# Other prices in a list scheduler, and a lock for VectorE and GpSimd: a two-layer decoder trunk on one core

## The chip, the core and the metric

The kernel runs on one NeuronCore of a Trainium2 chip. Five engines work side by side, each with its own queue, in order: TensorE (PE; its weight loads are listed as PEld), VectorE (DVE), ScalarE (ACT), GpSimd (POOL) and SyncE (SP), which issues most of the DMAs. The metric is the time of one execution on the device, in microseconds, lower is better. TensorE's clock has two levels, 2.4 and 1.2 GHz; the profile shows the granted share of the first (1.00 or 0.50, or a mean of them).

## What is computed

A batch of one sequence of 512 tokens, with 16 meta tokens ahead of it, goes through two layers, in float32, width 1024. A layer is a feed-forward network (half weight), a mixer, and a second feed-forward network, each followed by a layer norm on the residual:

```python
h = _layer_norm(ALPHA * h + 0.5 * _swiglu(h, wg0, wu0, wd0), g0, b0)      # 1024 -> 2816 -> 1024
lru_u, lru_y, ssd_z, ssd_xbc, ssd_dt, dn_qkv, ... = split(h @ w_in)       # 1024 -> 2832
mix = concat([rg_lru(...), mamba2_ssd(...), gated_deltanet(...)]) @ w_out
h = _layer_norm(ALPHA * h + mix, g1, b1)
h = _layer_norm(ALPHA * h + 0.5 * _swiglu(h, wg1, wu1, wd1), g2, b2)
```

The three parts of the mixer are recurrences over the tokens: the gated delta rule and the SSD in chunks of 64, with a state that is handed from chunk to chunk, the RG-LRU as a scan. The meta tokens are dropped from the output.

## The kernel before, in words

The tokens are worked in two halves: half 0 has 272 (16 meta, 256 others), half 1 has 256. Activations lie with the features on the partitions. A float32 product is made of three matmuls in a faster format, with weights and activations split into a high and a low part (`gemm`): high by high, low by high, high by low. These are the "g" matmuls, 128 x 128 weights by 256 or 272 columns, 24 for each product of 1024 inputs; in the trace `g<-hh,wt`, `g<-hl,wt` and `g<-hid,wt`. A weight slab of 512 KB is loaded to `wr` by SP, its high part cast by ACT, and the low part subtracted by POOL (in four pieces of 128 x 256) or by DVE (one of 128 x 1024), all into a tile `wt`.

The mixer's other matmuls are small and in plain float32; they write tiles "c". Per half they come as follows. `times` makes the step sizes (`dt_g`, `st_adt`) from a projection and its transposes (`sm`, `smd`, `mt`). `dn_pre`, `dn_solve`, `dn_post` and `dn_scan` do the delta rule: per-block matrices (`db`, `d_blk`), a triangular solve on DVE, its extension by blocks (`d_c`, `db`), and a scan with the state `d_s` (`d_r`, `d_wv`). `ssd_block` does the SSD: transposes of `acc`, decay matrices from `st_adt` and `tri`, masks on DVE, ACT and POOL (tiles `s`), and sums into `acc` and the state `s_st`. `lru` holds two gate matmuls (`wgate`, `l_h`) and the scan. `dn_finish` and `ssd_finish` normalise (`d_sq`, `s_sv`, `lq`). `layer_norm` sums the columns with a matmul of ones by `ls`, centres and squares on DVE, ACT and POOL (`ls2`, `lq`), sums the squares, takes a reciprocal square root in a chain of small DVE operations on `lv`, spreads the result with matmuls `ident,lv`, and writes `hh` and `hl`.

To keep PE at work, `Trunk.program` runs half 0's mixer beside half 1's feed-forward network, and the other way round, in an order given by a table (`KNOTS`, in `weave`). That order is only the recording: the calls go to a `Recorder`, whose queues hold operations with the tiles that they read and write. `levels` gives each operation the length of the longest priced path behind it. `schedule` then plays the five engines by the prices: it picks the engine that can start first, and on it the operation that is ready in the plan with the lowest class and the longest path; a "c" operation on PE and the operations around the PSUM tiles stand in the class ahead of the g matmuls. A result counts as usable on another engine after a lag from a table (`LAG`, plus `MARGIN`). PE's price doubles in the plan where its own count of columns says that the clock is low, and in long pauses it plans filler matmuls of ones. The order that comes out is issued to the engines as it is (`manual_schedule`), so each engine works it off in that order on the chip, and waits where the plan was wrong.

The prices are in `price`, per engine and kind of operation. In the profile of this kernel all operations have the line L390, in which the recorder issues them, and the fillers L388.

## Time and profile before

| | us |
|---|---|
| median of 3 runs (lowest to highest) | 2460.74 (2446.69 to 2464.13) |
| the profiled execution | 2460.38 |
| its span, first to last instruction | 2458.7 |
| PE busy in the span | 2312.6 (94%) |
| DVE / ACT / POOL busy | 1504.2 / 865.9 / 883.0 |
| mean granted clock of TensorE | 0.948 |

The feed-forward stretches lie from 0 to about 370, from 890 to 1560 and from 2090 us on; the first layer's mixer lies from about 370 to 890 us and the second's from 1560 to 2090. A busy PE is not a PE at its peak, since matmuls are pipelined and their ends are modelled. A wait is put down to the operation that came last.

### The profile page before, as it was taken

To read this page: it belongs to the slowest core of one execution; us is meant where nothing else is said; L and a number is where in the kernel's file an instruction comes from. 1 tells how busy PE (TensorE), PEld (TensorE's weight loads), DVE (VectorE), ACT (ScalarE), POOL (GpSimd) and SP (SyncE) were. 2 spreads that over 40 slices of the span, in tenths; PEclk is the share of its full clock that TensorE was granted. 3 is DMA by queue.
4 is the path that set the end of the run, shared out by engine and by line. 5 is a ranking of instruction groups with operands and counts; after the bars stand their busy time and mean duration, and the time that the engine had idled before them with its cause. 6 is when DMAs were issued, how large, how long until landed. Compare 5 with 4: busy or idle time off the path is not lost.

```text
span 2458.7 us, 46832 instructions
## 1 busy us (share of the span) xinstructions
PE 2312.6 (94%) x18712; PEld 2199.1 (89%) x18712; DVE 1504.2 (61%) x3529; ACT 865.9 (35%) x1546; POOL 883.0 (36%) x1214
## 2 busy tenths in 40 slices
PE   8999998988899999999999999998989989999997
PEld 8999998876887999999999999988768878999996
DVE  6444467757867664444574444678577686654445
ACT  3222344442333454222242223443433444432222
POOL 5000566634545576000010005666445556640000
PEclk9999999987886999999999999999888989999999
DMA  6232454531341456233232334545314525552320
GB/s 169 78 103 87 131 145 144 146 97 35 110 108 54 139 157 186 86 104 95 68 95 80 91 91 138 156 139 141 97 35 118 142 61 155 172 168 90 91 90 35
DMA packets 426332, 271.99 MB, mean 111 GB/s; under 512 B 33421, under 2 KB 407921, under 8 KB 425857
## 3 DMA queue, kind: packets, MB, share of 16 engines
q1 hardware_dynamic: 425536, 268.83, 37.7%
q8 instruction: 147, 2.41, 0.4%
q0 software_dynamic: 576, 0.16, 0.1%
q14 instruction: 73, 0.59, 0.1%
HBM read 260.76 MB, written 8.19 MB: 109 GB/s over the span
## 4 chain that ended last, share of the span: by engine, by line
PE 70%; DVE 16%; DMA 4%; issue 3%; POOL 3%; ACT 3%; SPq 0%; POOLq 0%; DVEq 0%; ACTq 0%
PE g L390 61%; PE c L390 9%; POOL wt L390 2%; DVE wt L390 2%; DVE acc L390 2%; DVE fs L390 1%; DVE lru L390 1%; ACT wt L390 1%; DMA wr<-in_ffn_w_gate_dram 1%; DVE d_sq L390 1%; DVE s L390 1%; DMA wr<-in_ffn_w_up_dram 1%; DMA d_tx<-d_xd 1%; DVE sp L390 1%; DVE l_h L390 1%
## 5 line engine op out<-in xcount | busy, mean ns | idle before, releaser
L390 PE MATMUL g<-hh,wt 128*128 128x256 f32 (+1 forms) x7616 | 1063.7, 290 | 22.5 <-DVE fs L390 8.8
L390 PEld LDWEIGHTS g<-hh,wt 128*128 128x128 f32 x7616 | 985.4, 192 | 37.5 <-DVE fs L390 9.0
L390 POOL TENSOR_TENSOR wt<-wr,wt 128x256 fp32r<-128x256 f32 x884 | 681.8, 803 | 783.7 <-ACT wt L390 726.4
L390 ACT CAST wt<-wr 128x1024 fp32r<-128x1024 f32 x484 | 498.0, 1040 | 619.0 <-PE g L390 482.0
L390 PE MATMUL g<-hl,wt 128*128 128x256 f32 (+1 forms) x3808 | 562.7, 288 | 1.8 <-DVE hl L390 1.2
L390 PE MATMUL g<-hid,wt 128*128 128x256 f32 (+1 forms) x4224 | 543.7, 286 | 18.6 <-DVE hid L390 10.2
L390 PEld LDWEIGHTS g<-hid,wt 128*128 128x128 f32 x4224 | 524.4, 189 | 27.2 <-DVE hid L390 13.0
L390 PEld LDWEIGHTS g<-hl,wt 128*128 128x128 f32 x3808 | 505.3, 192 | 6.3 <-DVE hl L390 2.5
L390 DVE SCALAR_TENSOR_TENSOR acc<-g,acc 128x256 f32<-128x256 f32 (+1 forms) x608 | 256.7, 427 | 226.1 <-PE g L390 222.0
L390 DVE TENSOR_TENSOR wt<-wr,wt 128x1024 fp32r<-128x1024 f32 x263 | 335.0, 1285 | 88.1 <-ACT wt L390 86.8
L390 DVE SCALAR_TENSOR_TENSOR fs<-ft,g 128x272 f32<-128x272 f32 (+1 forms) x200 | 84.6, 423 | 188.8 <-ACT ft L390 188.0
L390 DVE TENSOR_TENSOR g<-fs,g 128x256 f32<-128x256 f32 (+1 forms) x176 | 76.4, 434 | 173.9 <-PE g L390 173.5
L390 ACT ACTIVATE ft<-g 128x272 f32<-128x272 f32 (+1 forms) x208 | 80.6, 388 | 281.6 <-PE g L390 249.2
L390 ACT CAST hid<-g 128x256 fp32r<-128x256 f32 (+1 forms) x176 | 65.8, 374 | 223.5 <-DVE g L390 223.2
L390 POOL TENSOR_TENSOR ls<-ls,lq 128x256 f32<-128x256 f32 (+1 forms) x30 | 27.6, 920 | 264.2 <-ACT lq L390 261.3
L390 DVE TENSOR_TENSOR hid<-g,hid 128x256 fp32r<-128x256 f32 (+1 forms) x176 | 74.9, 425 | 42.4 <-ACT hid L390 42.1
L390 POOL TENSOR_TENSOR wr<-wr,db 128x512 f32<-128x512 f32 x4 | 5.0, 1274 | 262.0 <-ACT wr L390 262.0
L390 DVE SCALAR_TENSOR_TENSOR fs<-g,par,fs 128x271 f32<-128x271 f32 (+1 forms) x144 | 69.1, 482 | 21.9 <-ACT halo L390 17.0
L390 ACT ACTIVATE fs<-g,par 128x272 f32<-128x272 f32 (+1 forms) x48 | 25.2, 524 | 67.4 <-PE g L390 57.9
L390 DVE SCALAR_TENSOR_TENSOR acc<-acc,par,c 128x256 f32<-128x256 f32 (+1 forms) x104 | 43.6, 480 | 8.6 <-PE c L390 8.5
L390 ACT ACTIVATE ft<-fs 128x272 f32<-128x272 f32 (+1 forms) x56 | 23.7, 423 | 58.6 <-DVE fs L390 58.6
L390 POOL TENSOR_TENSOR s<-s,s_sm 128x512 f32<-128x512 f32 (+1 forms) x20 | 22.0, 1105 | 61.6 <-ACT s L390 45.1
(305 smaller groups left out, 1742.4 us busy)
## 6 DMA issues: line engine op xcount, KB each, us to landing
wr<-in_ffn_w_gate_dram SPq DMA_DIRECT2D x120, 512.0 KB
wr<-in_ffn_w_up_dram SPq DMA_DIRECT2D x120, 512.0 KB
wr<-in_ffn_w_down_dram SPq DMA_DIRECT2D x120, 512.0 KB
wr<-in_w_in_dram SPq DMA_DIRECT2D x88, 512.0 KB
wr<-in_w_out_dram SPq DMA_DIRECT2D x32, 512.0 KB
res<-acc SPq DMA_DIRECT2D x2, 1088.0 KB
acc<-res SPq DMA_DIRECT2D x8, 272.0 KB
acc<-in_x_dram SPq DMA_DIRECT2D x4, 512.0 KB
```

The costliest lines, as they stand in the source:

```text
L390: op.fn(*[on(x) for x in op.args], **{k: on(x) for k, x in op.kw.items()})
```

## The change

The prices of the plan change, and the plan gets one more rule. A matmul costs 12.5 ns beside its columns instead of 2.5 (`GAP`); in the half-clock case the columns alone double. A DMA is planned at 300 bytes per ns instead of 360. The lag from PE to ACT is 225 ns instead of 197. New is a lock: `shares` says which operations use the way into SBUF that DVE and POOL share: all of POOL's but memsets and DMAs, and on DVE those with more than one input tensor in SBUF (scalars not counted) and the copies, memsets and operations with a scalar that have all operands in SBUF. When such an operation is placed, the other engine's may start, in the plan, no sooner than its end less 90 ns (POOL behind DVE) or 160 ns (DVE behind POOL); until then it goes back and another ready operation is taken. Nothing else changes; no instruction of the program is added or removed, except that 57 fillers are planned and not 59.

```diff
--- before.py
+++ after.py
@@ -56,7 +56,7 @@
 class Op:
 
 
-    __slots__ = ("eng", "fn", "args", "kw", "cost", "load", "done", "cls", "prev", "preds", "succs", "level", "left", "ready", "seq", "tiles", "cols", "start", "after")
+    __slots__ = ("eng", "fn", "args", "kw", "cost", "load", "done", "cls", "prev", "preds", "succs", "level", "left", "ready", "seq", "tiles", "cols", "start", "after", "port")
 
 
 class Slots:
@@ -84,9 +84,9 @@
 
 
     PE, DVE, ACT, POOL, SP = range(5)
-    TICK, FULL, PAIR = 10240 / 3, 0.3735, 40
+    TICK, FULL, PAIR, GAP = 10240 / 3, 0.3735, 40, 12.5
     LAG = (
-        (0, 196, 197, 196, 189),
+        (0, 196, 225, 196, 189),
         (60, 127, 128, 155, 120),
         (210, 142, 142, 165, 135),
         (110, 76, 75, 104, 87),
@@ -125,14 +125,14 @@
         n = self.size(a[0])
         if name == "dma_start":
             b = n * a[0].ap[0][1] * 4
-            return (1040 if eng == self.POOL else 475), b / 360.0
+            return (1040 if eng == self.POOL else 475), b / 300.0
         if eng == self.PE:
             w, x = (a[1], a[2])
             fast = w.dtype == F32R
             c = (1 if fast else 2 if name == "transpose" else 4) / 2.4
             if self.region(a[0])[0] and self.size(w) <= 64:
                 return self.PAIR, 55
-            return self.size(x) * c + 2.5, self.size(w) * c
+            return self.size(x) * c + self.GAP, self.size(w) * c
         wide = max(self.size(x) for x in a)
         psum = any(x.space == bass.MemoryType.PSUM for x in a)
         if eng == self.DVE:
@@ -149,6 +149,15 @@
             return 36 + 0.85 * n * (2 if name == "affine_select" else 1), 0
         return (120 + 3.33 * n if name == "tensor_copy" else 148 + 2.1 * n), 0
 
+    def shares(self, eng, name, args):
+
+        sb = [x.space != bass.MemoryType.PSUM for x in args if hasattr(x, "ap") and self.size(x) > 1]
+        if eng == self.POOL:
+            return name not in ("memset", "dma_start")
+        if eng != self.DVE:
+            return False
+        return sum(sb[1:]) > 1 or name in ("tensor_scalar", "tensor_copy", "memset") and all(sb)
+
     def add(self, eng, name, fn, args, kw):
 
         t = args[0].tensor.name
@@ -168,7 +177,8 @@
         op = Op()
         op.eng, op.fn, op.args, op.kw, op.cls, op.seq = eng, fn, args, kw, self.cls, len(self.ops)
         op.cost, op.load = self.price(eng, name, args, kw)
-        op.cols = (op.cost - 2.5) * args[1].ap[0][1] / P if eng == self.PE and op.cost != self.PAIR else 0
+        op.cols = (op.cost - self.GAP) * args[1].ap[0][1] / P if eng == self.PE and op.cost != self.PAIR else 0
+        op.port = self.shares(eng, name, args)
         op.preds, op.tiles = set(), set()
         outs = [args[0]] + ([kw["accum_out"]] if kw.get("accum_out") is not None else [])
         ins = [x for x in list(args[1:]) + list(kw.values()) if hasattr(x, "ap")]
@@ -274,6 +284,7 @@
         lags = [[g + m for g, m in zip(r, MARGIN)] for r in self.LAG]
         free, now = [0.0] * 5, [0.0] * 5
         last_load = dma = 0.0
+        port = [0.0] * 5
         busy = [self.TICK] + [0.0] * 2000
         pending = [[] for _ in range(5)]
         ready = [[] for _ in range(5)]
@@ -302,6 +313,9 @@
                 op = self.ops[heapq.heappop(pending[e])[1]]
                 heapq.heappush(ready[e], (key(op), op.seq))
             op = self.ops[heapq.heappop(ready[e])[1]]
+            if op.port and port[e] > s:
+                heapq.heappush(pending[e], (port[e], op.seq))
+                continue
             new = [t for t in op.tiles if t not in owned]
             if new:
                 assert len(new) == 1
@@ -332,13 +346,16 @@
                         t += w
                 c, w = op.cost, op.load
                 if busy[int((s + w) // self.TICK)] < self.FULL * self.TICK:
-                    c, w = 2 * c, 2 * w
+                    c, w = 2 * (c - (self.GAP if op.cost != self.PAIR else 0)), 2 * w
                 op.start = s = max(s, last_load + w, op.ready + w)
                 last_load = s
                 busy[int(s // self.TICK) + 1] += op.cols
                 s += c - op.cost
             end = s + op.cost
             free[e] = end
+            if op.port:
+                q, early = (self.POOL, 90) if e == self.DVE else (self.DVE, 160)
+                port[q] = end - early
             if op.fn.__name__ == "dma_start":
                 dma = max(dma, end + 650) + op.load
                 end = dma
```

The operations come out in another order on all engines. On PE, in the first layer's mixer, half 0, from the fillers (`ones`) ahead of the end of the layer norm of half 1 (`lv`) into the SSD blocks (`acc`, `st_adt`). The numbers behind c_ and g_ are buffers. Before:

```order
L388 MATMUL c_123<-ones_104 128x128 x2
L390 MATMUL c_123<-ident_96,lv_876 128x128 x2
L390 MATMUL c_121<-ident_96,acc_24_119 16x128 x4
L390 MATMUL c_122<-ident_96,acc_24_119 16x128
L390 MATMUL c_122<-acc_24_119 16x16
L390 MATMUL c_123<-acc_24_119 16x16
L390 MATMUL c_121<-tri_105,st_adt_635 128x16 x2
L390 MATMUL c_122<-tri_105,st_adt_635 128x16
```

With the change, from the end of the same layer norm (the line number of the issue is L407):

```order
L407 MATMUL c_122<-ident_96,lv_876 128x128 x2
L407 MATMUL c_121<-ident_96,acc_24_119 16x128 x4
L407 MATMUL c_123<-ident_96,acc_24_119 16x128
L407 MATMUL c_123<-acc_24_119 16x16
L407 MATMUL g_145<-hl_4_99,wt_142 128x272 x5
L407 MATMUL g_136<-hh_2_97,wt_156 128x272 x16
L407 MATMUL g_136<-hl_4_99,wt_156 128x272 x8
L407 MATMUL c_122<-acc_24_119 16x16
L407 MATMUL g_139<-hh_2_97,wt_135 128x272 x15
L407 MATMUL c_121<-tri_105,st_adt_635 128x16 x2
L407 MATMUL c_123<-tri_105,st_adt_635 128x16
```

Before, the next g matmul comes behind all of the SSD blocks' 89 matmuls; with the change 125 g matmuls stand among them. Between the layer norm's first matmul (`c<-ls,ones`) and `lv` stand 116 g matmuls before, 27 with the change.

On PE, in the second layer's mixer, half 1, where the delta rule's scan (`d_wv`) ends and the SSD blocks begin. Before:

```order
L390 MATMUL g_139<-hh_3_98,wt_135 128x256 x6
L390 MATMUL c_123<-tri_105,st_adt_998 128x128 x4
L390 MATMUL g_139<-hh_3_98,wt_135 128x256 x4
L390 MATMUL g_139<-hl_5_100,wt_135 128x256 x5
L390 MATMUL c_125<-ls_565,ones_104 128x256
L390 MATMUL g_139<-hl_5_100,wt_135 128x256 x3
L390 MATMUL g_136<-hh_3_98,wt_156 128x256
L390 MATMUL c_124<-s_814_909,s_st_907 64x128
L390 MATMUL c_124<-s_808_903,s_799_894 64x128
```

With the change:

```order
L407 MATMUL c_125<-ident_96,acc_32_127 128x128
L407 MATMUL c_125<-acc_32_127 128x128
L407 MATMUL c_124<-acc_32_127 128x128
L407 MATMUL c_121<-tri_105,st_adt_998 128x128 x4
L407 MATMUL c_123<-d_wv_760,db_652 64x64 x2
L407 MATMUL g_136<-hh_3_98,wt_156 128x256 x2
L407 MATMUL g_136<-hl_5_100,wt_156 128x256 x3
L407 MATMUL c_125<-ls_565,ones_104 128x256
L407 MATMUL c_124<-s_814_909,s_st_907 64x128
L407 MATMUL c_124<-s_808_903,s_799_894 64x128
```

Here g matmuls went out from between the small ones: from the first `d_c` matmul of this half to its layer norm's end (`lv`) 131 stand before, 62 with the change, and 40 more of them stand ahead, between `dt_g` and `d_c`. Three more counts of the same kind, on PE: between the first mixer's transposes of step sizes (`sm`) and `dt_g`, 82 g matmuls before and 171 with the change; among the SSD blocks of the second mixer's half 0, 12 and 73; over the layer norm ahead of these, 130 and 82.

## Rows read from the trace of the kernel before

**Rows 1.** The page: its first line, the span and the instructions in it.

```profile
span 2458.7 us, 46832 instructions
```

**Rows 2.** The stretches of 100 us (busy time and count of each engine; granted clock; DMA).

```profile
500.00:600.00 100.00, 88.53 (x662) 68.87 (x662) 64.83 (x166) 36.10 (x81) 35.23 (x48) 0.81 0.20 54
1100.00:1200.00 100.00, 100.00 (x821) 100.00 (x820) 45.39 (x81) 23.09 (x38) 0.00 (x0) 1.00 0.30 90
1900.00:2000.00 100.00, 92.28 (x840) 78.99 (x838) 69.36 (x196) 39.73 (x78) 53.98 (x71) 0.91 0.39 104
```

**Rows 3.** The page, section 4: the chain that ended last, by engine.

```profile
PE 70%; DVE 16%; DMA 4%; issue 3%; POOL 3%; ACT 3%; SPq 0%; POOLq 0%; DVEq 0%; ACTq 0%
```

**Rows 4.** Stretches of the first mixer, 517 to 590 us, and their sum.

```profile
530.00:545.00 15.00, 8.89 (x64) 8.19 (x65) 12.09 (x30) 8.19 (x19) 6.64 (x10) 0.80 0.52 141
545.00:560.00 15.00, 13.14 (x55) 9.14 (x55) 8.52 (x31) 5.03 (x12) 3.50 (x5) 0.50 0.20 70
560.00:575.00 15.00, 15.00 (x51) 8.10 (x51) 6.25 (x13) 1.41 (x4) 1.47 (x3) 0.50 0.00 1
575.00:590.00 15.00, 12.09 (x78) 8.81 (x78) 12.50 (x30) 3.55 (x7) 5.72 (x6) 0.95 0.00 1
sum 73.00, PE 62.11 PEld 46.71 DVE 46.14 ACT 25.66 POOL 24.93; mean PE 12.42 PEld 9.34 DVE 9.23 ACT 5.13 POOL 4.99
```

**Rows 5.** Timeline of PE (start, length, operation, count), the layer norm's first matmul.

```profile
517.22 0.70 PE L390 MATMUL c<-ls,ones 128*128 128x256 f32 x2
```

**Rows 6.** Timeline of PE, the same layer norm's last matmuls.

```profile
537.17 0.71 PE L390 MATMUL c<-ident,lv 128*128 128x128 f32 x4 [2.25 <-DVE lv L390]
```

**Rows 7.** Timeline of PE, another layer norm, its first and last matmuls.

```profile
1245.65 0.63 PE L390 MATMUL c<-ls,ones 128*128 128x256 f32 x2
1258.76 0.71 PE L390 MATMUL c<-ident,lv 128*128 128x128 f32 x4 [0.60 <-DVE lv L390]
```

**Rows 8.** Timeline of DVE, the operations on lv (3 elements a partition).

```profile
532.73 1.15 DVE L390 TENSOR_SCALAR lv<-lv 128x3 int32<-128x3 int32 x2
533.91 0.65 DVE L390 TENSOR_TENSOR lv<-lv 128x3 f32<-128x3 f32 x1
534.60 1.33 DVE L390 SCALAR_TENSOR_TENSOR lv<-lv 128x3 f32<-128x3 f32 x2
536.17 0.36 DVE L390 SCALAR_TENSOR_TENSOR lv<-lv 128x3 f32<-128x3 f32 x2
```

**Rows 9.** Timeline of POOL over the same stretch.

```profile
531.04 4.87 POOL L390 TENSOR_TENSOR wt<-wr,wt 128x256 fp32r<-128x256 f32 x7
```

**Rows 10.** The tile lv: one kind of operation, min/median/max ns.

```profile
L390 DVE SCALAR_TENSOR_TENSOR lv<-lv x60: 145/163/703, 356.8 to 2093.8; 128x3 f32<-128x3 f32 x60
```

**Rows 11.** Waits of PE, 370 to 500 us (us in total, times, longest).

```profile
PE c L390 <- DVE db L390: 4.4, 3, 1.8
PE c L390 <- DVE d_blk L390: 4.3, 5, 1.6
PE c L390 <- DVE dt_g L390: 2.8, 1, 2.8
```

**Rows 12.** Waits of PE, 780 to 825 us.

```profile
PE c L390 <- DVE ls L390: 3.8, 1, 3.8
PE c L390 <- DVE d_sq L390: 3.2, 1, 3.2
```

**Rows 13.** Stretches of the second mixer, half 0, 1768 to 1812 us.

```profile
1768.00:1783.00 15.00, 12.37 (x57) 9.75 (x58) 7.59 (x28) 5.04 (x13) 8.19 (x9) 0.50 0.37 116
1783.00:1798.00 15.00, 13.43 (x74) 8.24 (x72) 10.04 (x25) 4.66 (x9) 2.63 (x4) 0.94 0.00 1
1798.00:1812.00 14.00, 9.80 (x37) 5.00 (x38) 7.88 (x18) 1.47 (x3) 4.35 (x5) 0.64 0.00 0
```

**Rows 14.** Stretches of the second mixer, half 1, 1925 to 2010 us: the sum.

```profile
sum 85.00, PE 76.57 PEld 63.18 DVE 54.77 ACT 33.62 POOL 38.27; mean PE 12.76 PEld 10.53 DVE 9.13 ACT 5.60 POOL 6.38
```

**Rows 15.** Waits of all engines, whole run: the weight casts for a DMA.

```profile
ACT wt L390 <- DMA wr<-in_ffn_w_gate_dram: 27.3, 21, 3.3
```

## The prediction

> **What bounds the kernel now.** I read the page first, then the run in stretches of 100 us, then the chain of waits, and last the timelines and the waits of the stretches that were slow. The span is 2458.7 us [rows 1]. In the feed-forward stretches TensorE (PE) is the bound and loses nothing: between 1100 and 1200 us it is busy for all 100 us at a granted clock of 1.00 (2.4 GHz), 821 matmuls, so 121.8 ns for one "g" matmul, the mean of those with 256 and with 272 columns. In the two mixers it is different: the stretches from 500 and from 1900 us have a granted clock of 0.81 and 0.91 and PE busy 88.5 and 92.3 us of 100 [rows 2]. The chain of waits says the same: 70% of it is PE, but 16% is VectorE (DVE) [rows 3]. So what an edit of the order can win or lose lies in the mixers, and it shows there as idle PE and as time at 1.2 GHz.
>
> The worst place is in the first mixer, where the layer norm of token half 1 and the SSD blocks of half 0 follow each other. From 530 to 590 us PE is busy for 49.1 us (8.89 + 13.14 + 15.00 + 12.09), so 10.9 us idle; the granted clocks 0.80, 0.50, 0.50 and 0.95 mean 6.0 + 15.0 + 15.0 + 1.5 = 37.5 us at 1.2 GHz. DVE is busy for 46.1 of the 73 us from 517 [rows 4]. What PE did before the clock fell: hardly any g matmul is in that stretch, only small fp32 ones.
>
> **The change part by part.** No instruction of the program is added or removed but two of the 59 filler matmuls (0.2 us each, so nothing); prices act only through the order. Some 4,200 of PE's 17,214 operations stand at another place, on DVE 2,117 of 3,529, on ScalarE 602 of 1,545, on GpSimd (POOL) 535 of 1,210, on SP 131 of 609 DMAs, the last by 14 places at most. I go by PE and DVE, place by place, and count g matmuls between two named instructions in the two orders, at 0.1218 us each.
>
> The price of a matmul was columns / 2.4 GHz + 2.5 ns, 109.2 ns for 256 columns and 115.8 for 272; now 119.2 and 125.8. The 121.8 ns of the trace [rows 2] lie between the new prices and above both old ones. The Trainium skill (TensorE: Matmul & The Clock Gate, "Wait — 56ns, not 53.3ns?") speaks against this part: it gives columns / 2.4 GHz plus about 2.5 ns for back-to-back bf16 matmuls, the old price. By it the 125 g matmuls below would be worth 14.5 us and not 15.2; the row is of this kernel's matmuls and decides.
>
> Place 1, first mixer, half 0. The matmul that opens the layer norm starts at 517.22 [rows 5], the one that ends it at 537.17 [rows 6]: 20.0 us, over which the old order lays 116 g matmuls (14.1 us), and none between there and the end of the SSD blocks. The new order lays 27 (3.3 us) over the layer norm and 125 (15.2 us) among the SSD blocks. The layer norm: the shortest in the trace takes 13.1 us, 1245.65 to 1258.76 [rows 7]. So this part takes 13.1 to 20.0 us, with PE standing for 10 to 17 us of it, a new wait. The SSD part, 537 to 590, takes 53 us. With full clock its PE work would be 49.1 less half of 37.5, 30.4 us, and with the 15.2 us of g, less some 3 that ran before 537, 42 us from 530; so at best 18 us less, at worst none. DVE's 39.4 us of work in those windows [rows 4] would still fit. Bounds for the place: 25 us less (7 + 18) to 5 us more (the clock falls during the layer norm's new wait). I take 9 us less: a layer norm halfway, and 6 us of the SSD, nearer to no gain than to the best, since DVE does its work in order and PE's waits there are for DVE.
>
> Within that stretch DVE also waits for POOL. Five operations on 3 elements of "lv" take 1.15 + 0.65 + 1.33 us from 532.73 to 535.93, the next ones 0.18 each [rows 8], while POOL runs seven pieces of 0.70 us back to back [rows 9]; over the trace such an operation takes 163 ns in the median and 703 at most [rows 10]. So the collision costs some 2.3 us of this layer norm. The new lock moves work around such pieces in the plan; nothing in the order shows fewer pieces beside the chains, so I put its gain at 0, and price it as a rival. The Trainium skill (SBUF — State Buffer, "Who interferes with whom") says that a VectorE instruction with two SBUF inputs and a GpSimd instruction that reads SBUF exclude each other, the second to issue blocking fully, and that the order of issue decides who loses. The rows agree: 0.65 us is about one piece.
>
> Place 2, first mixer, half 0 before its solve. PE's waits between 370 and 500 us that DVE ends come to 11.5 us: 4.4 for db, 4.3 for d_blk, 2.8 for dt_g [rows 11]. The new order lays 89 more g matmuls (10.8 us) between the transposes of the step sizes and dt_g, so that wait of 2.8 us goes; the others shrink in part. Bounds: 11.5 us less to 4 more (the chain behind starts later). I take 4 less.
>
> Place 3, end of the first mixer: 3.8 and 3.2 us of waits for ls and d_sq [rows 12], both consumers later in the new order. Bounds 7 less to 2 more; 2 less.
>
> Place 4, second mixer, half 0, the same blocks as place 1: 73 g matmuls among them where 12 were; over the layer norm 82 where 130 were. From 1768 to 1812 PE is idle for 8.4 us of 44, and 26.9 us are at 1.2 GHz [rows 13]. The best is 8.4 + 13.5 = 21.9 us less, scaled by the cover it gets (61 of 125) 11; the worst 3 more. I take 5 less.
>
> Place 5, second mixer, half 1: the new order goes the other way. Between the first d_c matmul and the end of the layer norm stand 62 g matmuls instead of 131, and 40 more run ahead of it. That is 8.4 us of cover gone from a stretch in which PE is busy 76.6 of 85 us and DVE 54.8 [rows 14]. Bounds: 4 less (fewer g matmuls in front of the chain's own) to 16 more (8.4, and the clock for a third of the stretch). I take 5 more.
>
> The DMA price (512 KB in 1.75 us where it was 1.46) and the 28 ns on PE to ScalarE I put at 0: the longest kind of wait of the weight casts for a DMA is 27.3 us in 21 pieces, none over 3.3 [rows 15], on an engine that is busy for a third of the span; if that cover went, those 27 us are spread over the whole run and PE has loaded tiles ahead.
>
> Sum: -9 - 4 - 2 - 5 + 5 = -15 us. The profiled execution took 2460.38 us, so **2445 us**; the median of the runs, 2460.74, is 0.4 above it.
>
> **The rivals.** *The lock pays* (2425 us): the collisions leave the chains. Ten layer norms at 2.3 us [rows 8, 10] are 23 us at most; half of that, 11, and place 1 at 18 less instead of 9, give 2425. For it: ten groups of such small operations on chains that PE waits for. Against: POOL's pieces come with the weight slabs and their number is the same.
>
> *Nothing moves* (2459 us): DVE's in-order work sets the pace of the mixers, PE's waits change place only. For it: DVE is the releaser in nearly all waits of [rows 11, 12]. Against: at place 1 it is busy for 46 of 73 us, so it has room.
>
> *The bare chain* (2488 us), slower: at place 5 PE now has small matmuls almost alone, as at place 1 before, and the clock falls there as it did there: 37.5 us at 1.2 GHz [rows 4] cost 18.8 us, and the 8.4 us of cover are lost too, so 27 us more; the layer norm at place 1, with 17 us of PE standing, eats what the SSD blocks win. It decides if more than 20 us of place 5 run at 1.2 GHz. Against: 62 g matmuls are left.
>
> **How the numbers follow.** Forecast 0.42, lock pays 0.20, nothing 0.20, bare chain 0.18. About 1% (24.6 us: 2436 and 2485) is what a measurement of this kernel tells from no change. The forecast's own range is 2430 to 2462, by the bounds above taken not all at one end; three in ten of it lie below 2436. Faster: 0.42 x 0.3 + 0.20 x 0.9 + 0.20 x 0.05 = 0.32. Slower: 0.18 x 0.7 + 0.03 for the rest = 0.15. Within 1%: 0.53. The range that leaves out 2 in 10 runs from 2416 (lock case with place 2 and 4 at their better ends) to 2486.
>
> **What would show it.** Place 1: g matmuls among the SSD matmuls, far less than 37.5 us at 1.2 GHz, and a wait of PE for lv of 5 us or more. Place 2: no wait for dt_g. Place 4: a clock nearer to 1 in its three windows. Place 5: a lower clock, longer waits for s and lv. The lock's case: an "lv" median unchanged but few of 600 ns. The forecast is wrong if place 1 keeps its length, or if new waits of the same size stand elsewhere in the mixers.

## The result, and the profile after

The changed kernel takes 2423.2 us (median of 4 runs, 2418.8 to 2424.9), the kernel before, run again beside it, 2458.2 us: a ratio of 0.9863 with a 95% interval of 0.9832 to 0.9893, so 35 us or 1.4% faster. The forecast was 2445, the range 2416 to 2486; the forecast's own range, 2430 to 2462, did not reach so low. The profiled execution took 2422.22 us, 38.2 less than the one of before.

The page's span, the stretches that answer to [rows 2] (busy time and count of each engine, granted clock, DMA), and the chain's shares by engine that answer to [rows 3]:

```profile
span 2420.5 us, 46856 instructions
```

```profile
500.00:600.00 100.00, 95.41 (x657) 78.36 (x655) 71.57 (x190) 39.48 (x87) 46.86 (x61) 0.81 0.23 64
1100.00:1200.00 100.00, 98.83 (x802) 97.87 (x801) 53.21 (x103) 24.57 (x43) 2.72 (x3) 1.00 0.27 80
1900.00:2000.00 100.00, 87.54 (x630) 70.01 (x630) 69.67 (x209) 37.27 (x81) 35.21 (x43) 0.76 0.20 58
```

```profile
PE 68%; DVE 15%; DMA 5%; issue 4%; ACT 4%; POOL 4%; SPq 0%; POOLq 0%; DVEq 0%; ACTq 0%
```

The same hundred microseconds hold other work now, so the counts of matmuls can't be compared, but one thing can be read: in the feed-forward stretch, where PE was busy for all 100 us before, it is busy for 98.83. The mean granted clock rose from 0.948 to 0.960, so the time at 1.2 GHz fell from 256 us (2 x 0.052 x 2458.7) to 194 (2 x 0.040 x 2420.5).

**Where the time went.** Fixed times are no good for two orders, so I cut both traces at named instructions of PE, in each mixer: the first matmul of the four layer norms (`c<-ls,ones`), the first `d_c` matmul of each half, and the last `s_bt` matmul of half 0's SSD blocks. PE's *loss* in such a stretch is its length less what PE's instructions in it take back to back at 2.4 GHz, each at the lower quartile of its shape's spacing in the trace of before. That work is 2106 us in both. Fillers count as work. Loss in us, first / second mixer:

| stretch | before | after |
|---|---|---|
| A: first norm to d_c of half 0 (place 2) | 25.0 / 25.9 | 14.3 / 18.4 |
| B: d_c to the second norm | 12.5 / 12.2 | 19.2 / 11.6 |
| C: second norm to the last s_bt (places 1, 4) | 26.0 / 21.6 | 15.3 / 10.4 |
| D: from there to d_c of half 1 | 30.2 / 33.8 | 23.5 / 29.1 |
| E: d_c to the third norm (place 5, first part) | 30.6 / 8.3 | 21.5 / 10.7 |
| F: third norm to the fourth (places 3, 5) | 20.0 / 27.3 | 16.8 / 35.3 |
| all else (feed-forward, head, end) | 78.7 | 88.2 |

A and D together give 29.7 us, B and C 15.7, E and F 1.8; the rest of the program takes 9.5 back.

**Place 1.** Stretches of the first mixer, answering to [rows 4]:

```profile
490.00:505.00 15.00, 12.91 (x149) 10.75 (x147) 6.71 (x22) 1.90 (x5) 0.00 (x0) 0.60 0.08 6
505.00:520.00 15.00, 14.28 (x97) 12.11 (x97) 8.64 (x27) 5.86 (x16) 4.53 (x7) 0.50 0.01 2
520.00:535.00 15.00, 14.98 (x108) 13.67 (x108) 12.33 (x43) 8.94 (x22) 6.17 (x7) 0.87 0.41 106
535.00:550.00 15.00, 14.24 (x94) 10.16 (x93) 12.13 (x23) 6.15 (x14) 9.03 (x12) 1.00 0.37 107
550.00:565.00 15.00, 12.82 (x87) 9.90 (x87) 10.56 (x26) 6.12 (x11) 6.90 (x8) 0.99 0.24 67
565.00:580.00 15.00, 14.14 (x62) 9.72 (x60) 8.32 (x23) 1.91 (x6) 4.13 (x6) 0.55 0.15 39
```

PE's layer norm, first and last matmuls (start, length), answering to [rows 5, 6]; then DVE's operations on lv in it and POOL's piece beside them, answering to [rows 8, 9]:

```profile
510.42 1.22 PE L407 MATMUL c<-ls,ones 128*128 128x256 f32 x2
522.10 1.22 PE L407 MATMUL c<-ident,lv 128*128 128x128 f32 x4
```

```profile
518.91 0.88 DVE L407 TENSOR_SCALAR lv<-lv 128x3 int32<-128x3 int32 x2
519.82 0.64 DVE L407 TENSOR_TENSOR lv<-lv 128x3 f32<-128x3 f32 x1
520.50 0.36 DVE L407 SCALAR_TENSOR_TENSOR lv<-lv 128x3 f32<-128x3 f32 x2
```

```profile
517.66 2.79 POOL L407 TENSOR_TENSOR wt<-wr,wt 128x256 fp32r<-128x256 f32 x4 [1.20 <-ACT wt L407]
```

The norm takes 11.7 us, under the 13.1 of [rows 7], with 27 g matmuls over it and no wait of PE for lv. The SSD blocks behind it run at 0.87, 1.00 and 0.99. But the low clock has not gone: it moved ahead, to 490 to 523, when PE works on the delta rule's small matmuls, and a piece stays at 565.

The tile lv over the whole trace, the same kind of operation as [rows 10]:

```profile
L407 DVE SCALAR_TENSOR_TENSOR lv<-lv x60: 100/164/698, 357.4 to 2053.8; 128x3 f32<-128x3 f32 x60
```

**Place 2.** Before, PE's wait for dt_g and the stretch right behind it, which ran at 1.2 GHz:

```profile
388.68 0.44 PE L390 MATMUL c<-tri,dt_g 64*64 64x64 f32 x2 [2.76 <-DVE dt_g L390]
```

```profile
388.70:398.90 10.20, 10.20 (x67) 9.13 (x68) 4.00 (x20) 4.57 (x16) 6.00 (x9) 0.50 0.49 156
```

After, the stretch from the first norm to the first d_c matmul, and PE's waits in it (total, times, longest), where [rows 11] had 2.8 us for dt_g:

```profile
346.00:473.00 127.00, 120.94 (x1003) 115.03 (x1003) 110.06 (x314) 61.42 (x119) 90.61 (x135) 0.99 0.53 149
```

```profile
PE c L407 <- DVE db L407: 2.0, 2, 1.1
PE c L407 <- POOL mt L407: 1.5, 1, 1.5
PE g L407 <- DVE fs L407: 0.8, 1, 0.8
PE c L407 <- DVE d_blk L407: 0.6, 1, 0.6
```

**Places 4 and 5**, answering to [rows 13] and [rows 14] (for 5 first before, then after; the granted clock is the last but two):

```profile
1712.00:1727.00 15.00, 14.98 (x120) 14.28 (x120) 12.66 (x39) 9.51 (x23) 7.22 (x14) 1.00 0.40 106
1727.00:1742.00 15.00, 13.84 (x105) 12.62 (x106) 10.13 (x34) 9.57 (x22) 10.68 (x11) 0.89 0.59 176
1742.00:1757.00 15.00, 11.88 (x69) 6.97 (x67) 11.67 (x30) 5.92 (x11) 7.83 (x10) 1.00 0.13 36
1757.00:1765.00 8.00, 7.82 (x34) 4.08 (x34) 4.02 (x8) 0.00 (x0) 1.66 (x3) 0.65 0.00 0
```

```profile
1925.00:2010.00 85.00, 76.57 (x695) 63.18 (x695) 54.77 (x156) 33.62 (x73) 38.27 (x50) 0.88 0.33 90
```

```profile
1883.00:1968.00 85.00, 74.89 (x605) 57.59 (x604) 47.05 (x139) 26.59 (x58) 31.64 (x41) 0.76 0.24 66
```

Place 4 had 0.50, 0.94 and 0.64; now it has 1.00, 0.89 and 1.00 until its last eight microseconds at 0.65. Place 5 went the other way, as forecast: a clock of 0.76 over its 85 us, where it was 0.88.

### The profile page after: what moved, and what is told of

Same layout as the page of the kernel before. It is cut to its first block, busy times and chain, and to the rows that moved or that the text cites. A ratio compares the mean times of both kernels' runs of the same rounds, so it can differ in the third digit from the quotient of the medians.

```text
span 2420.5 us, 46856 instructions
## 1 busy us (share of the span) xinstructions
PE 2293.7 (95%) x18708; PEld 2181.7 (90%) x18708; DVE 1492.4 (62%) x3529; ACT 866.1 (36%) x1546; POOL 889.7 (37%) x1214
## 4 chain that ended last, share of the span: by engine, by line
PE 68%; DVE 15%; DMA 5%; issue 4%; ACT 4%; POOL 4%; SPq 0%; POOLq 0%; DVEq 0%; ACTq 0%
PE g L407 59%; PE c L407 9%; POOL wt L407 3%; DVE wt L407 3%; ACT wt L407 2%; DMA wr<-in_ffn_w_up_dram 2%; DVE acc L407 1%; DVE fs L407 1%; DVE s L407 1%; DMA wr<-in_ffn_w_gate_dram 1%; DVE d_ss L407 1%; DVE db L407 1%; DVE ls L407 1%; DVE lru L407 1%; DVE d_sq L407 1%
## 5 line engine op out<-in xcount | busy, mean ns | idle before, releaser
L407 PE MATMUL g<-hh,wt 128*128 128x256 f32 (+1 forms) x7616 | 1063.3, 290 | 24.5 <-ACT hh L407 13.5
L407 PEld LDWEIGHTS g<-hh,wt 128*128 128x128 f32 x7616 | 985.3, 192 | 39.4 <-ACT hh L407 16.1
L407 POOL TENSOR_TENSOR wt<-wr,wt 128x256 fp32r<-128x256 f32 x884 | 687.0, 810 | 743.5 <-ACT wt L407 705.9
L407 ACT CAST wt<-wr 128x1024 fp32r<-128x1024 f32 x484 | 497.9, 1041 | 622.6 <-PE g L407 479.5
L407 PE MATMUL g<-hid,wt 128*128 128x256 f32 (+1 forms) x4224 | 548.4, 287 | 25.6 <-DVE hid L407 13.6
L407 PEld LDWEIGHTS g<-hid,wt 128*128 128x128 f32 x4224 | 526.7, 190 | 36.7 <-DVE hid L407 18.8
L407 PE MATMUL g<-hl,wt 128*128 128x256 f32 (+1 forms) x3808 | 557.8, 287 | 1.5 <-POOL hl L407 1.5
L407 PEld LDWEIGHTS g<-hl,wt 128*128 128x128 f32 x3808 | 500.7, 190 | 5.6 <-POOL hl L407 1.9
L407 DVE SCALAR_TENSOR_TENSOR acc<-g,acc 128x256 f32<-128x256 f32 (+1 forms) x608 | 256.0, 428 | 226.5 <-PE g L407 222.6
L407 DVE TENSOR_TENSOR wt<-wr,wt 128x1024 fp32r<-128x1024 f32 x263 | 334.1, 1281 | 97.4 <-ACT wt L407 95.1
L407 DVE SCALAR_TENSOR_TENSOR fs<-ft,g 128x272 f32<-128x272 f32 (+1 forms) x200 | 84.7, 424 | 181.4 <-ACT ft L407 180.6
L407 ACT ACTIVATE ft<-g 128x272 f32<-128x272 f32 (+1 forms) x208 | 80.8, 389 | 303.2 <-PE g L407 258.3
L407 DVE TENSOR_TENSOR g<-fs,g 128x256 f32<-128x256 f32 (+1 forms) x176 | 76.3, 434 | 173.5 <-PE g L407 173.2
L407 ACT CAST hid<-g 128x256 fp32r<-128x256 f32 (+1 forms) x176 | 65.8, 374 | 202.5 <-DVE g L407 202.2
L407 POOL TENSOR_TENSOR ls<-ls,lq 128x256 f32<-128x256 f32 (+1 forms) x30 | 26.3, 875 | 303.0 <-ACT lq L407 299.5
L407 DVE TENSOR_TENSOR hid<-g,hid 128x256 fp32r<-128x256 f32 (+1 forms) x176 | 75.2, 427 | 47.0 <-ACT hid L407 46.9
L407 POOL TENSOR_TENSOR wr<-wr,db 128x512 f32<-128x512 f32 x4 | 5.0, 1280 | 266.4 <-ACT wr L407 266.4
L407 DVE SCALAR_TENSOR_TENSOR fs<-g,par,fs 128x271 f32<-128x271 f32 (+1 forms) x144 | 69.5, 484 | 15.3 <-ACT halo L407 10.2
L407 DVE SCALAR_TENSOR_TENSOR acc<-acc,par,c 128x256 f32<-128x256 f32 (+1 forms) x104 | 44.2, 482 | 8.4 <-PE c L407 8.3
L407 ACT ACTIVATE fs<-g,par 128x272 f32<-128x272 f32 (+1 forms) x48 | 25.1, 524 | 63.0 <-PE g L407 58.0
L407 POOL TENSOR_TENSOR s<-s,s_sm 128x512 f32<-128x512 f32 (+1 forms) x20 | 25.4, 1274 | 57.3 <-ACT s L407 54.3
L407 ACT ACTIVATE hh<-acc,par 128x256 fp32r<-128x256 f32 (+1 forms) x80 | 35.2, 505 | 25.3 <-DVE acc L407 25.3
```

Source lines behind the costliest of these rows:

```text
L407: op.fn(*[on(x) for x in op.args], **{k: on(x) for k, x in op.kw.items()})
```

## The experiments

Four theories stood against each other. *Prices*: what wins is where the plan puts g matmuls, and the matmul's price decides that. *Apart*: the lock keeps DVE's and POOL's operations from meeting on the chip. *Slow chains*: the lock pays because the plan learns that chains through DVE and POOL are slow, and lays more g matmuls ahead of what reads them. *Reshuffle*: any touch of a price gives another order, with a time of its own. (The first expectations call the second one the lock theory; the third came after the first four runs.) Ratios are to the kernel before, run on the same chip.

**1. Without the lock.**

```diff
-            if op.port and port[e] > s:
-                heapq.heappush(pending[e], (port[e], op.seq))
-                continue
```

> The changed prices without the lock. The changed kernel ran 2423 us, the one before 2458. Prices theory (what wins is where the plan puts g matmuls, and the price of a matmul decides that): 2420 to 2432, nearly the whole gain stays. Lock theory (what wins is that small VectorE operations no longer meet GpSimd's pieces): 2445 or more, and the operations on lv over 500 ns are near the 19 of before, not the 7 of the changed kernel. Reshuffle theory (any touch of a price makes another order, and each order has a time of its own, spread over some 20 us whatever the touch means): anywhere from 2415 to 2460.

Measured: 2466.0 us, ratio 1.0032 (1.0009 to 1.0054), slower than before; 17 operations on lv over 500 ns. The prices alone win nothing: that theory falls.

**2. The lock alone** (before's prices).

```diff
-    TICK, FULL, PAIR, GAP = 10240 / 3, 0.3735, 40, 12.5
+    TICK, FULL, PAIR, GAP = 10240 / 3, 0.3735, 40, 2.5
-        (0, 196, 225, 196, 189),
+        (0, 196, 197, 196, 189),
-            return (1040 if eng == self.POOL else 475), b / 300.0
+            return (1040 if eng == self.POOL else 475), b / 360.0
```

(and the half-clock line as before)

> The kernel before with the lock alone; its prices are the old ones. Prices theory: 2450 to 2460. Lock theory: 2425 to 2440, with at most 8 operations on lv over 500 ns. Reshuffle theory: 2415 to 2460; the plan lays 23 g matmuls over the layer norm of place 1 and none over the next one, so place 1 should gain and the end of the first mixer lose.

Measured: 2434.0 us, 0.9909 (0.9873 to 0.9946). The lock wins by itself, but with 16 operations on lv over 500 ns, not 8: the time is the lock theory's, the sign that it named is not there. Reshuffle's range holds the time too, and both of its signs came: in the first mixer stretch C lost about 11 us less than before, F about 12 more.

**3. The matmul's price alone**: the changed kernel without the three lines of the lock, and

```diff
-        (0, 196, 225, 196, 189),
+        (0, 196, 197, 196, 189),
-            return (1040 if eng == self.POOL else 475), b / 300.0
+            return (1040 if eng == self.POOL else 475), b / 360.0
```

> The kernel before with the matmul's price alone changed (12.5 ns beside the columns). Prices theory: 2420 to 2435. Lock theory: 2445 to 2460. Reshuffle theory: 2415 to 2460.

Measured: 2480.0 us, 1.0108 (1.0072 to 1.0144): above the range of every theory, reshuffle's too.

**4. The kernel before with a DMA at 355 bytes per ns.**

```diff
-            return (1040 if eng == self.POOL else 475), b / 360.0
+            return (1040 if eng == self.POOL else 475), b / 355.0
```

> The kernel before with one price touched by 1.4%: a DMA at 355 bytes per ns instead of 360. It means nothing for any theory of prices or of the lock, which both expect 2450 to 2460 (no change). But the order comes out another: over the layer norm of place 1 the plan now lays 21 g matmuls where the kernel before lays 116 and the changed one 27; over the next layer norm 20 where 92 and 59 stand. Reshuffle theory: the time differs from the kernel before by 8 us or more, and place 1's layer norm takes 12 to 14 us as in the changed kernel (11.7), not 20.

Measured: 2438.2 us, 0.9938 (0.9915 to 0.9961). A price that means nothing moved the time by 0.6%. Place 1's norm went with it, first and last matmuls:

```profile
511.64 1.22 PE L404 MATMUL c<-ls,ones 128*128 128x256 f32 x2
521.51 1.23 PE L404 MATMUL c<-ident,lv 128*128 128x128 f32 x4 [0.77 <-DVE lv L404]
```

9.9 us (12 to 14 were expected) with 21 g matmuls over it, and stretch C lost 16.5 us for 26.0, with no lock. So place 1's gain belongs to the order that leaves g matmuls for the SSD blocks, and several touches reach it.

**5. No lock, but dearer operations.**

```diff
         op.port = self.shares(eng, name, args)
+        if op.port:
+            op.cost += 125 if eng == self.DVE else 100
```

(without the three lines of the lock)

> No lock; the other prices as in the changed kernel. Instead every operation that the lock would cover costs more in the plan: 125 ns on VectorE, 100 ns on GpSimd, which is what they take on average in the trace of before over the shortest of their kind (183 us in 1433 operations, and 118 us in about 1130). Slow-chain theory (the lock pays because the plan learns that the chains through VectorE and GpSimd are slow, and lays the matmuls that read them later): 2423 to 2440. Apart theory (it pays because operations of the two engines are kept from meeting): 2455 or more, as without the lock (2466).

Measured: 2450.8 us, 0.9961 (0.9937 to 0.9985): between the two, by ratio 17 us under the kernel without the lock (1), not the 41 that the lock is worth there. Its profiled execution, 2431.3, was its fastest, 19 us under its median, so its places below look better than its usual execution.

**6. The lock chooses, but costs no time.**

```diff
             if op.port and port[e] > s:
-                heapq.heappush(pending[e], (port[e], op.seq))
-                continue
+                rest = [x for x in ready[e] if not self.ops[x[1]].port]
+                if rest:
+                    ready[e].remove(min(rest))
+                    ready[e].append((key(op), op.seq))
+                    heapq.heapify(ready[e])
+                    op = self.ops[min(rest)[1]]
```

> The lock chooses but costs no time: an operation that it covers steps back only if one that needs no shared way is ready on its engine at that moment, which then goes; else it is placed at once. In the plan of the changed kernel the lock held an operation of VectorE back 1315 times, and only in 3 of them such another was ready (GpSimd: 59 of 834). Slow-chain theory: 2455 to 2475, as without the lock (2466). Apart theory, in the form that the choice is what matters: 2420 to 2440.

Measured: 2456.3 us, 0.9994 (0.9975 to 1.0013). By ratio 9 us under (1): most of what the lock is worth comes with the time that it takes in the plan. The choice alone had little to choose from: by the expectation's count another operation was ready in 62 of 2149 cases, and up to the first `c<-tri,dt_g` the order lays as many g matmuls as (1), 275.

**7. The changed kernel with one lag 1 ns longer.**

```diff
-        (0, 196, 225, 196, 189),
+        (0, 196, 226, 196, 189),
```

> The changed kernel with one lag touched by 1 ns (PE to ScalarE 226 for 225); it means nothing, but the order comes out another (over the layer norm of the second mixer's half 0 28 g matmuls where the changed kernel lays 82, over that of half 1 57 where it lays 21). If an order's time is spread by chance as among the kernels without the lock (2438 to 2480): 2405 to 2445. If the lock and the prices decide: within 6 us of 2423.

Measured: 2431.4 us, 0.9883 (0.9858 to 0.9907), 5 us from the changed kernel in ratio.

**8. Matmul's price and lock**, without the other two.

```diff
-        (0, 196, 225, 196, 189),
+        (0, 196, 197, 196, 189),
-            return (1040 if eng == self.POOL else 475), b / 300.0
+            return (1040 if eng == self.POOL else 475), b / 360.0
```

> The matmul's price and the lock, without the DMA's price and the lag to ScalarE. If the DMA's price and the lag are worth nothing (my forecast had them at 0): 2415 to 2435. Without the lock they went with 14 us less (2480 to 2466); if that is an effect and not chance, 2430 to 2445 here.

Measured: 2458.1 us, 0.9989 (0.9972 to 1.0006). Neither expectation: 13 us above the upper end of the worse one. Taken from the changed kernel, the two prices that I had put at 0 cost it the whole gain.

**9. DMA's price and lag alone**, in the kernel before.

```diff
-        (0, 196, 197, 196, 189),
+        (0, 196, 225, 196, 189),
-            return (1040 if eng == self.POOL else 475), b / 360.0
+            return (1040 if eng == self.POOL else 475), b / 300.0
```

> The kernel before with the DMA's price and the lag to ScalarE alone. If these are an effect (with the matmul's price changed they went with 14 us less without the lock and 35 us less with it): 2425 to 2442. If they only reshuffle: 2440 to 2475, and the wait of PE for dt_g at place 2 stays at 2.5 us or more as in every kernel without the lock so far.

Measured: 2451.5 us, 0.9990 (0.9965 to 1.0016): nothing by themselves.

**10. The changed kernel with the old matmul price** (and the half-clock line as before).

```diff
-    TICK, FULL, PAIR, GAP = 10240 / 3, 0.3735, 40, 12.5
+    TICK, FULL, PAIR, GAP = 10240 / 3, 0.3735, 40, 2.5
```

> The changed kernel with the old price of a matmul (2.5 ns beside the columns). The old price is 10 ns too low, which leaves room ahead of what PE waits for: the stretch from the first layer's second mixer norm on (730 us of PE's work to 1300) took 6 to 9 us longer in every kernel with the new price than in the kernel before. If the lock, the DMA's price and the lag add up: 2400 to 2420, faster than the changed kernel. If the new price is needed, or the DMA's price does nothing: 2430 to 2440. No wait for dt_g of over 1 us at place 2 by either.

Measured: 2445.1 us, 0.9959 (0.9936 to 0.9982): neither the sum nor the lock's own 0.9909.

**11. The changed kernel with 8 ns.**

```diff
-    TICK, FULL, PAIR, GAP = 10240 / 3, 0.3735, 40, 12.5
+    TICK, FULL, PAIR, GAP = 10240 / 3, 0.3735, 40, 8.0
```

> The changed kernel with a matmul's price of 8 ns beside the columns instead of 12.5. If the price works steadily, between the changed kernel's 2423 and the old price under the same lock: 2410 to 2430. If an order's time is chance within the locked kernels (2423 to 2458 so far): 2415 to 2455.

Measured: 2426.0 us, 0.9874 (0.9842 to 0.9907), not told apart from the changed kernel. No version here beats it.

**12. The lock as long as the blocker's price.**

```diff
-                q, early = (self.POOL, 90) if e == self.DVE else (self.DVE, 160)
+                q, early = (self.POOL, 0) if e == self.DVE else (self.DVE, 0)
```

> The changed kernel with the lock as long as the blocker's whole price (0 for the 90 and 160 ns). If the lock pays by making the plan's chains slower, a longer lock moves the matmuls still farther back: the plan lays 201 g matmuls over the layer norms at the mixers' ends where the changed kernel lays 143 and 160, and 181 fillers are planned for 57, so PE has too little left elsewhere: 2430 to 2460. If it pays by keeping operations apart, the excess of VectorE's operations falls by more than the 12 us of the changed kernel, and the time is 2405 to 2423.

Measured: 2464.6 us, 1.0043 (1.0022 to 1.0064): a longer lock loses all. That is 5 us above the slow-chain theory's range and far above the apart theory's; ahead of dt_g this plan lays fewer g matmuls than the changed kernel's, 345 for 399.

**What they say together.** The eight settings of lock, matmul price and DMA price with lag are all measured, ratios without and with the lock:

| matmul price, DMA price and lag | no lock | lock | difference |
|---|---|---|---|
| old, old | 1 | 0.9909 | -0.0091 |
| old, new | 0.9990 | 0.9959 | -0.0031 |
| new, old | 1.0108 | 0.9989 | -0.0119 |
| new, new | 1.0032 | 0.9863 | -0.0169 |

The lock wins in all four, 1.0% or 25 us in the mean (0.3 to 1.7%). The matmul's price changes sign (+0.0108, +0.0042, +0.0080, -0.0096), and so do the DMA's price and lag (-0.0010, -0.0076, +0.0050, -0.0126). A meaningless touch moves 0.2 to 0.6% (7, 4), so of the differences between single cells no more than the lock's mean can be named with ease.

*Collisions do not set the time.* Every kernel has the same operations on DVE, so its busy time shows how long they took, those that met POOL's among them. Of the pages, in this order: before (2458), after (2423), the lock alone (2434), price and lock (2458), the lag of 226 (2431), the full lock (2465):

```profile
PE 2312.6 (94%) x18712; PEld 2199.1 (89%) x18712; DVE 1504.2 (61%) x3529; ACT 865.9 (35%) x1546; POOL 883.0 (36%) x1214
```

```profile
PE 2293.7 (95%) x18708; PEld 2181.7 (90%) x18708; DVE 1492.4 (62%) x3529; ACT 866.1 (36%) x1546; POOL 889.7 (37%) x1214
```

```profile
PE 2309.3 (95%) x18798; PEld 2202.3 (91%) x18798; DVE 1485.0 (61%) x3529; ACT 871.7 (36%) x1546; POOL 884.8 (36%) x1214
```

```profile
PE 2311.9 (94%) x18784; PEld 2198.4 (90%) x18784; DVE 1487.0 (61%) x3529; ACT 866.9 (35%) x1546; POOL 885.2 (36%) x1214
```

```profile
PE 2302.8 (95%) x18704; PEld 2191.4 (90%) x18704; DVE 1504.9 (62%) x3529; ACT 867.3 (36%) x1546; POOL 886.9 (36%) x1214
```

```profile
PE 2316.6 (94%) x18956; PEld 2212.6 (90%) x18956; DVE 1491.1 (61%) x3529; ACT 870.0 (35%) x1546; POOL 893.8 (36%) x1214
```

The lag of 226 keeps the gain with 1504.9 us, no less than before; the two of the six that gain nothing have 13 and 17 us less than before. In the four pairs of the table the lock does lower DVE's busy time, from 1504.2 to 1485.0 us, 1509.5 to 1490.8, 1503.5 to 1487.0 and 1500.8 to 1492.4, but the last pair, which gains most in time, has the smallest fall. So fewer collisions may give a part of the lock's gain; they don't decide its size.

*Where the lock's gain lies: in the chain ahead of the delta rule.* Loss of PE in stretches A and D of both mixers, and outside the mixers, with the g matmuls that the order lays between the first norm's first matmul and the first `c<-tri,dt_g`, first mixer (the full lock's stretches overlap, so it is left out):

| kernel | A + D, us | g ahead of dt_g | outside, us |
|---|---|---|---|
| before | 114.9 | 292 | 78.7 |
| 9, DMA and lag | 113.5 | 300 | 75.2 |
| 4, DMA 355 | 104.9 | 322 | 81.6 |
| 6, choice only | 115.6 | 275 | 95.1 |
| 1, no lock | 119.1 | 275 | 95.2 |
| 3, matmul price | 113.0 | 260 | 104.5 |
| 5, dearer | 94.1 | 386 | 80.0 |
| after | 85.2 | 399 | 88.2 |
| 7, lag 226 | 87.2 | 399 | 91.7 |
| 8, price and lock | 83.4 | 397 | 94.6 |
| 2, lock alone | 89.7 | 435 | 72.8 |
| 10, lock and DMA | 99.6 | 527 | 66.8 |
| 11, price 8 | 97.4 | 340 | 72.6 |

Without the lock 105 to 119 us are lost there, with it 83 to 100, and with dearer operations 94, in that one fast execution. The other profiled executions lie within 8 us of their medians. The fillers in A and D, were they counted as loss, would add 5 to 8 us to (2), (5), (8) and (10) and at most 1.5 to the others.

Taken in the four pairs of lock and no lock, in the order of the table above, A and D lose 25.2, 13.9, 29.6 and 33.9 us less with the lock (19, 9, 23 and 32 with fillers as loss), beside 22, 8, 29 and 42 us of time: the same ranking, and nearly the same mean. This is the strongest sign that the lock's gain lies there. Over the whole run PE waits 8.1 to 10.2 us for dt_g in the kernels with neither lock nor dearer operations, 5.2 in (5), and 0.9 to 3.2 in the seven with the lock. Near 390 us (11), as fast as the changed kernel, still has 2.5 us of it, so that single wait is not the gain. PE's waits for dt_g near 390 us, in the kernels without the lock (1), with the matmul's price alone (3), with DMA and lag alone (9), and with the lock and a lag of 226 (7); the changed kernel and the lock alone have none there:

```profile
PE c L404 <- DVE dt_g L404: 2.9, 1, 2.9
```

```profile
PE c L404 <- DVE dt_g L404: 3.6, 2, 3.3
```

```profile
PE c L404 <- DVE dt_g L404: 5.6, 2, 5.3
```

```profile
PE c L407 <- DVE dt_g L407: 0.4, 1, 0.4
```

## Why the prediction held, and where it did not

The range held the time and all five places moved the way that they were said to. The size did not hold: 35 us for 15. That the range reached down to 2416 it owed to the lock's case, not to the sum, whose own range ended at 2430. The five places as they were counted give 25.4 of the 37.7 us of loss that went; the rest is the balance of stretches that the sum had at nothing. Stretch by stretch, in loss:

- Place 1, -9: C lost 10.7 us less. But B, ahead of it, lost 6.7 more, since the low clock moved there, and the wait for lv of 5 us or more did not come: the norm took 11.7 us, less than the 13.1 that I had as its least (its first five operations on lv 1.88 us for 3.13, beside four of POOL's pieces for seven), and PE's work over it, at 0.50 from 505 to 520 us, took longer than I had counted. "Far less than 37.5 us at 1.2 GHz" holds for the SSD blocks alone. And what PE did before the clock fell was not read right: from 530 to 539 us, 28 of its 49 matmuls are g, and then it stood 2.25 us for lv [rows 6]; the stretch without a g matmul is that at 1.2 GHz, 539 to 576.
- Place 2, -4: **this is the term that was mis-sized.** A lost 10.7 us less, near the better bound of 11.5. I had counted a wait of 2.8 us and part of two others; with the wait went the low clock behind it (10 us of A at 1.2 GHz before, 3 after). And I counted it in one place of four: A of the second mixer gave 7.5 us, the two D 6.7 and 4.7, which the sum had at nothing.
- Place 3, -2: 3.2; the E ahead of it, not in the sum, 9.1. The wait for ls of 3.8 us [rows 12] is now

```profile
PE c L407 <- DVE ls L407: 1.8, 1, 1.8
```

- Place 4, -5: 11.2. Place 5, +5: 10.4 (2.4 and 8.0). Its waits for s grew from 2.3 to 4.1 us, as said; those for lv did not, 0.6 for 1.8. The condition of the rival *the bare chain* came: 41 us of its 85 at 1.2 GHz (2 x 0.24 x 85), over the 20 that were named. It cost 10 us and not 27, since 20 were at 1.2 GHz before, and the other places won more.
- The lock, 0: put at nothing because "nothing in the order shows fewer pieces beside the chains". The places counted the order that the lock had made, but the sum didn't see that this order hangs on it: without the lock the same prices win nothing (1), and the lock is worth 25 us in the mean of four pairs, mostly through the time that it takes in the plan (6). The rival *the lock pays* came within 2 us of the time, and its sign came too: the median of one kind of operation on lv stayed (164 ns for 163), those over 500 ns fell from 19 to 7. But all operations on lv together fell from 31.3 to 24.4 us, 7 us and not 11, and by so much only in this kernel (11 to 16 over 500 ns in the others with the lock, 13 to 18 in those with neither lock nor dearer operations). The Trainium skill (SBUF — State Buffer, "Who interferes with whom") has a VectorE operation with two SBUF inputs and a GpSimd one that reads SBUF exclude each other; the rows fit that (0.64 us for one operation beside POOL's pieces of 0.70, 0.16 else). A plan that respects it made operations on lv over 500 ns rarer in each of the four pairs, from 19 to 16, 16 to 11, 13 to 11 and 17 to 7, but did not do away with them.
- The matmul's price: right as a price. These are 16 matmuls of 256 and 16 of 272 columns and what follows them:

```profile
1015.75 2.07 PE L407 MATMUL g<-hh,wt 128*128 128x256 f32 x16
1017.66 1.12 PE L407 MATMUL g<-hl,wt 128*128 128x256 f32 x8
...
1021.50 2.16 PE L407 MATMUL g<-hh,wt 128*128 128x272 f32 x16
1023.50 1.16 PE L407 MATMUL g<-hl,wt 128*128 128x272 f32 x8
```

At a granted clock of 1.00, 1.91 and 2.00 us for sixteen, 119.4 and 125.0 ns, against the new 119.2 and 125.8. (The 2.5 ns beside the columns of the Trainium skill, TensorE: Matmul & The Clock Gate, "Wait — 56ns, not 53.3ns?", is 12.7 and 11.7 here.) Yet I put its effect outside the mixers at nothing, and there it costs: 67 to 82 us are lost at 2.5 or 8 ns in the plan, 88 to 105 at 12.5 (80 in (5), where the chains are dearer too). PE's waits for hid in the feed-forward of the changed kernel, between 1000 and 1190 us, where PE waited for nothing before:

```profile
1047.90 15.59 PE L407 MATMUL g<-hid,wt 128*128 128x272 f32 x126 [0.49 <-DVE hid L407]
1101.46 15.57 PE L407 MATMUL g<-hid,wt 128*128 128x272 f32 x126 [0.48 <-DVE hid L407]
1155.03 15.59 PE L407 MATMUL g<-hid,wt 128*128 128x272 f32 x126 [0.49 <-DVE hid L407]
```

Over 900 to 1550 us, before and after:

```profile
PE g L390 <- DVE hid L390: 3.4, 4, 1.9
```

```profile
PE g L407 <- DVE hid L407: 6.8, 12, 1.3
```

That the low price was a margin for chains whose real lag is longer than the plan's is the reading that fits; no run changed that lag alone.

- DMA's price and lag, 0: right alone (9), not beside the other two (8). The weight casts wait longer for DMAs, 38.4 us for one kind where the longest was 27.3 [rows 15], on an engine with room (the line below). That isn't the new price's doing: all kinds together wait 91 us before, 103 in the changed kernel and 123 in (8), which has the lock with the old DMA price.

```profile
ACT wt L407 <- DMA wr<-in_ffn_w_up_dram: 38.4, 28, 5.1
```

**What stays open.** Why (8) gains nothing against the kernel before. Beside (3), which has the same prices and no lock, it has the lock's gain whole (-0.0119); so the question is why the matmul's price costs 1.1% with the old DMA price and lag and wins 1.0% with the new ones under the lock. Against the changed kernel, (8)'s A and D are as good (83.4 us); it loses 15 us more at the mixers' ends (E and F 99.5 us for 84.4), as the lock with DMA price does (103.6), 6 more outside the mixers, and 38 more fillers take some 8. Whether the DMA's price keeps the ends good or an order met them by chance, runs of single orders with a spread of 0.6% don't tell. Nor was the new price in the mixers tried with the old one in the feed-forward, which the table would favour. And that the plan's time for the slow chains is what pays is in part argued: dearer operations (5) gave 17 us of 41, and a longer lock (12) lost. The DMA's price and the lag were not tested apart, but for the small touches of (4) and (7), nor, but for the 8 ns of (11), the matmul's price apart from its half-clock line.

## What to carry to other kernels

A list schedule's rule can pay in another way than the one that it was written for: read what it does to the plan's clock, and count the work that it lays ahead of the late chains. Where one place gains by such a rule, look for all its siblings (the other half, the other layer) before making a sum, and for the margin that a wrong price was. And touch a price that means nothing first: here it moved 0.6%, and a difference of that size from a single order proves no cause.

## What was not expected of the hardware

DVE's busy time follows the lock by little, and not always: 1500 to 1513 us in the seven kernels without it (the choice alone, (6), among them), 1485 to 1493 in six of the seven with it, and 1505 in (7), which differs from the changed kernel by 1 ns in one lag. And at place 1 the low clock was not removed by the work laid there: it fell at 539 to 576 us before and at 493 to 524 us after, ahead of the norm, when the delta rule's small matmuls had the engine, and once more from 565 on.
